# Second MLP product of a hybrid block: moving operand and PSUM result walked in another order of columns, one of eight orders for each bank

## The chip, the cores and the metric

The kernel runs on one core of one Trainium2 chip. The metric is the time of one execution on the device in microseconds (us); smaller is better. The time of the kernel before is the median of three runs.

## The reference, cut to what matters

One layer with parallel heads (an mLSTM group and a differential-attention group) is followed by an MLP. The change touches the last line of the reference only, the product with `w_ff2`:

```python
x = x + (mixed @ w_out[l]).astype(dt)
u = rms(x, norm2_g[l]).astype(dt) @ w_ff1[l]      # 1024 x 4096
u = jnp.square(jax.nn.relu(u))
x = x + (u @ w_ff2[l]).astype(dt)                 # 1024 x 1024
```

Here x is 1024 rows (sequence) by 1024 columns (model width), and `w_ff2` is 4096 by 1024. All is float32.

## The kernel before, in words

The stages follow each other on TensorE: projections, mLSTM, attention, the output projection, the first MLP product (lines 1435 to 1437, program name `m`), and the second MLP product (lines 1764 to 1766, program name `z`). The second MLP product is the last stage.

**How the second product is tiled.** Rows and columns of the result are split into halves, and the four quarter products are formed from seven products of sums and differences, numbered 1 to 7 and worked in the order 1, 6, 2, 5, 7, 3, 4. Each of the seven runs over eight steps j, a step over two blocks b of 128 of the contraction, and a block over four groups n of 128 output rows. So a step has 8 pairs (b, n), and each pair is three matmuls: the weights are cut into a high and a low part (`wh`, `wl`, float32r), the activations too (`gh`, `gl`), and high by high, high by low and low by high are added up. The weights are the stationary operand (128 by 128), the activations are the moving operand (128 partitions by 512 columns), and the result is one PSUM bank, 128 partitions by 512 columns of float32. In all there are 7 x 8 x 2 x 4 x 3 = 1344 matmuls, and each of the three lines issues 448 of them.

**Which bank.** `x = 4 * (i in (6, 5, 3))` chooses the banks: products 1, 2, 7 and 4 add into banks 0 to 3, products 6, 5 and 3 into banks 4 to 7, group n into bank x + n. A bank of 0 to 3 so receives 4 x 8 x 2 x 3 = 192 matmuls and a bank of 4 to 7 receives 3 x 8 x 2 x 3 = 144. Product 2 goes on in the sum of product 1, 3 in that of 5, and 4 in that of 7. A sum in a bank thus runs over 48 or 96 matmuls, and `finish` (lines 1795 and on) then reads the bank with ScalarE or VectorE, column by column, combines it with other sums, and the result goes out.

**The order of the work.** It is written out by hand: `when(t, f, ...)` collects a time in units of the schedule and a function, and the functions are called in order of time, so each engine's queue is in that order. For each step, `fetch` loads the activations from device memory (SyncE's queue), `cut_hi` makes the high part on ScalarE (line 1348) and `cut_lo` the low part on VectorE (line 1351), for the activations (`wb`, `we` in turn) and for the weights (`wa0`, `wa1` in turn); `z_step` issues the 24 matmuls.

## Time and profile before

| what | value |
|---|---|
| median of 3 runs | 1246.6 us |
| lowest and highest of them | 1244.84 and 1247.13 us |
| span of the profiled execution, first to last instruction | 1243.3 us |
| TensorE matmul, busy share of the span | 99% (6437 matmuls) |
| VectorE, ScalarE, GpSimd busy share | 67%, 50%, 19% |
| granted TensorE clock, mean | 1.000 |

For the profiled execution the profile gives the span only; the median of the timed runs lies 3.3 us above that span. In the profile the engines are named PE (TensorE's matmuls), PEld (its weight loads), DVE (VectorE), ACT (ScalarE), POOL (GpSimd) and SP (SyncE). A matmul's own duration is modelled at its end and overlaps the next matmul, so the pace of TensorE is read from the starts of successive matmuls. A row of a group reads: line, engine, operation, result<-operands, shapes, count, then busy time in us and mean ns of one, then the idle time of the engine before them and what ended it.

### The profile page before, as it was taken

The page shows a single profiled execution, that of the slowest core. Times are in us where ns is not written, and L with a number is a line of the kernel's source. Part 1 is how long each engine was busy: PE and PEld are TensorE (multiplying, and loading weights), DVE is VectorE, ACT ScalarE, POOL GpSimd, SP SyncE. Part 2 cuts the span into 40 slices and gives each one's busy share as a digit, 9 for nine tenths or more (in the row PEclk, how much of TensorE's full clock was granted, in tenths as well). Part 3 has the DMA queues.
Part 4 walks back from the last instruction along what each step waited for, and adds up shares of the span by engine and source line. Part 5 has one row for each costly group of instructions (what it writes and reads, how often), then busy time and mean ns, then how long its engine had stood idle before and what let it go on. Part 6 is the DMA issues. An engine that isn't in the chain of part 4 may idle for free. (4 is left out here: it accounts for less than half of the span.)

```text
span 1243.3 us, 17129 instructions
## 1 busy us (share of the span) xinstructions
PE 1235.1 (99%) x6437; PEld 1033.6 (83%) x6437; DVE 827.1 (67%) x1138; ACT 621.4 (50%) x1067; POOL 234.8 (19%) x259
## 2 busy tenths in 40 slices
PE   9999999999999999999999999999999999999998
PEld 8998778888878878888887888888888888888887
DVE  8335658886357786774879886666655874468754
ACT  7223437776455686664455554544534343333332
POOL 0133504564334364322000000000000000004001
PEclk9999999999999999999999999999999999999999
DMA  6404262354275485435544764434359745435632
GB/s 251 153 20 171 52 199 91 111 153 128 93 237 188 150 289 182 160 111 203 173 170 146 257 233 153 162 136 163 144 180 364 260 161 195 139 132 170 221 110 93
DMA packets 101314, 208.31 MB, mean 168 GB/s; under 512 B 8672, under 2 KB 21472, under 8 KB 101232
## 3 DMA queue, kind: packets, MB, share of 16 engines
q1 hardware_dynamic: 77936, 154.11, 37.2%
q10 hardware_dynamic: 15296, 31.89, 6.8%
q0 software_dynamic: 8000, 21.24, 5.2%
q8 instruction: 50, 0.82, 0.3%
q14 instruction: 32, 0.26, 0.1%
HBM read 148.90 MB, written 58.29 MB: 167 GB/s over the span
## 5 line engine op out<-in xcount | busy, mean ns | idle before, releaser
L1809 POOL TENSOR_TENSOR zx<-zx,res 128x512 f32<-128x512 f32 x4 | 8.7, 2179 | 491.0 <-DVE zx L1807 491.0
L1766 PE MATMUL z<-wbh,wa0l 128*128 128x512 f32 x224 | 87.4, 390 | 0.2 <-DVE wa0l L1351 0.2
L1003 DVE CUSTOM_DVE_ANT_0 l<-pl,toe 128x1024 f32<-128x1024 f32 x64 | 76.3, 1221 | 16.6 <-PE pl L998 15.9
L1765 PE MATMUL z<-wbl,wa0h 128*128 128x512 f32 x224 | 87.2, 389 | 0.0
L1765 PE MATMUL z<-wel,wa1h 128*128 128x512 f32 x224 | 87.2, 389 | 0.0
L1764 PE MATMUL z<-weh,wa1h 128*128 128x512 f32 x224 | 87.2, 389 | 0.0
L1764 PE MATMUL z<-wbh,wa0h 128*128 128x512 f32 x224 | 87.1, 389 | 0.0
L1766 PE MATMUL z<-weh,wa1l 128*128 128x512 f32 x224 | 87.1, 389 | 0.0
L1348 ACT ACTIVATE wbh<-g 128x1024 fp32r<-128x1024 f32 x28 | 29.7, 1061 | 90.3 <-PE z L1766 53.0
L1348 ACT ACTIVATE weh<-g 128x1024 fp32r<-128x1024 f32 x28 | 29.7, 1061 | 90.2 <-PE z L1766 53.4
L1009 ACT ACTIVATE l<-l,sm 128x1024 f32<-128x1024 f32 x64 | 73.1, 1148 | 0.5 <-DVE sm L1003 0.5
L1351 DVE TENSOR_TENSOR wel<-g,weh 128x1024 fp32r<-128x1024 f32 x28 | 35.2, 1258 | 56.5 <-ACT weh L1348 56.5
L1484 ACT ACTIVATE sq<-sq 128x512 f32<-128x512 f32 x48 | 30.2, 630 | 82.3 <-DVE sq L1523 65.7
L1351 DVE TENSOR_TENSOR wbl<-g,wbh 128x1024 fp32r<-128x1024 f32 x28 | 35.4, 1265 | 52.4 <-ACT wbh L1348 52.4
L1038 PEld LDWEIGHTS pav<-v,at 128*128 128x128 f32 x512 | 61.5, 191 | 3.4 <-issue 1.1
L1038 PE MATMUL pav<-v,at 128*128 128x128 f32 x512 | 62.7, 275 | 0.0
L998 PE MATMUL pl<-kk,q 64*128 64x512 f32 x384 | 55.3, 410 | 0.9 <-DVE sm L1003 0.9
L136 PE MATMUL pj_c<-hhi,w_c 128*128 128x512 f32 x128 | 53.3, 417 | 0.0
L136 PE MATMUL pw<-mix,hi_wo 128*128 128x512 f32 x128 | 52.0, 406 | 0.0
L138 PE MATMUL pj_c<-hhi,w_c 128*128 128x512 f32 x128 | 50.4, 394 | 0.0
L138 PE MATMUL pw<-mix,lo_wo 128*128 128x512 f32 x128 | 50.1, 391 | 0.0
L137 PE MATMUL pj_c<-hlo,w_c 128*128 128x512 f32 x128 | 50.0, 391 | 0.0
(456 smaller groups left out, 3592.5 us busy)
## 6 DMA issues: line engine op xcount, KB each, us to landing
g<-g_dram SPq DMA_DIRECT2D x56, 512.0 KB, 4.7
g_dram<-gs SPq DMA_DIRECT2D x64, 256.0 KB, 4.3
g_dram<-sq ACTq DMA_DIRECT2D x42, 256.0 KB, 2.1
kk<-k_dram POOLq DMA_DIRECT2D x16, 512.0 KB, 6.3
raw_wo<-in_w_o_dram SPq DMA_DIRECT2D x16, 512.0 KB, 4.5
re<-in_w_dram SPq DMA_DIRECT2D x16, 512.0 KB, 4.3
ro<-in_w_dram SPq DMA_DIRECT2D x16, 512.0 KB, 3.5
zt<-in_w_dram SPq DMA_DIRECT2D x16, 512.0 KB, 4.0
```

What stands on the lines that cost most here:

```text
L136: nc.tensor.matmul(out, ahi, bhi, start=start, stop=False)
L137: nc.tensor.matmul(out, ahi, blo, start=False, stop=False)
L138: latest[0] = nc.tensor.matmul(out, alo, bhi, start=False, stop=stop).ins
L998: nc.tensor.matmul(it.pl[x][:, sl], hd.q[r, i, qi * P : (qi + 1) * P], hd.kk[r, j, sl], start=n == 0, stop=n == 2)
L1003: nc.vector.tensor_tensor_reduce(lt, it.pl[m], hd.toe[:, off : off + S], 1.0, 3.0e38, ALU.add, ALU.min, it.sm[:, m : m + 1])
L1009: nc.scalar.activation(lt, lt, AF.Exp, bias=sm[:, m : m + 1], scale=-1.0, accum_out=sm[:, 2 + m : 3 + m])
L1038: nc.tensor.matmul(it.pav[:, 0:P], at, it.head.v[:, c], start=c == 0, stop=c == NC - 1)
L1348: nc.scalar.activation(dst[0][idx], src, AF.Copy)
L1351: nc.vector.tensor_tensor(dst[1][idx], src, dst[0][idx].bitcast(F32), op=ALU.subtract)
L1764: nc.tensor.matmul(p, wh, gh, start=go, stop=False, skip_group_check=True)
L1765: nc.tensor.matmul(p, wh, gl, start=False, stop=False, skip_group_check=True)
L1766: nc.tensor.matmul(p, wl, gh, start=False, stop=end, skip_group_check=True)
```

## The change: what it does

A helper `walk` is added, and one line in `z_step` puts it around the result `p` and the moving operands `gh` and `gl` of every matmul. The three get the same walk, so a column of the operand still lands in the same place of the bank; only the order in which the 512 columns are streamed differs. The weights, the number of matmuls, their columns and their order are as before.

```diff
+    def walk(t, n):
+
+        if n == 0:
+            return t
+        if n == 5:
+            return t[:, ::-1]
+        if n == 6:
+            return t.rearrange("p (h c) -> p h c", h=4)[:, ::-1]
+        return t.rearrange("p (h a b) -> p a h b", h=2, b={1: 4, 2: 2, 3: 32, 4: 16, 7: 8}[n])
...
             end = j == NJ - 1 and b == 1
+            p, gh, gl = (walk(t, x + n) for t in (p, gh, gl))
             nc.tensor.matmul(p, wh, gh, start=go, stop=False, skip_group_check=True)
```

What a bank's number gives:

| bank | order of the 512 columns | runs of adjacent columns | matmuls |
|---|---|---|---|
| 0 | ascending, as before | 1 of 512 | 192 |
| 1 | halves in turn | 128 of 4 | 192 |
| 2 | halves in turn | 256 of 2 | 192 |
| 3 | halves in turn | 16 of 32 | 192 |
| 4 | halves in turn | 32 of 16 | 144 |
| 5 | descending | 1 of 512, backwards | 144 |
| 6 | four quarters, the last first | 4 of 128 | 144 |
| 7 | halves in turn | 64 of 8 | 144 |

"Halves in turn" with runs of 2 means columns 0, 1, 256, 257, 2, 3, 258, 259 and so on.

On TensorE, at the start of product 1, these matmuls stand before (`z_n` is the bank's tile, `wbh` the high part of the activations, `wa0h` that of the weights; of the three lines of a group only the first is shown):

```order
L1764 MATMUL z_0_8393<-wbh,wa0h 128x512
...
L1764 MATMUL z_1_8394<-wbh,wa0h 128x512
...
L1764 MATMUL z_2_8395<-wbh,wa0h 128x512
...
L1764 MATMUL z_3_8396<-wbh,wa0h 128x512
...
L1764 MATMUL z_0_8393<-weh,wa1h 128x512
```

The same place on TensorE now, and the start of product 6 behind it (`z_0_8684` to `z_3_8687` are its banks 4 to 7):

```order
L1775 MATMUL z_0_8393<-wbh,wa0h 128x512
...
L1775 MATMUL z_1_8394<-wbh,wa0h 128x64x2x4
...
L1775 MATMUL z_2_8395<-wbh,wa0h 128x128x2x2
...
L1775 MATMUL z_3_8396<-wbh,wa0h 128x8x2x32
...
L1775 MATMUL z_0_8684<-wbh,wa0h 128x16x2x16
...
L1775 MATMUL z_1_8685<-wbh,wa0h 128x512
...
L1775 MATMUL z_2_8686<-wbh,wa0h 128x4x128
...
L1775 MATMUL z_3_8687<-wbh,wa0h 128x32x2x8
```

No matmul has moved: the shapes alone differ, and bank 5 keeps the shape 128x512 since its walk is one run backwards. The rows and the waits of VectorE, ScalarE, GpSimd and SyncE are the same as before.

## The prediction

> **What bounds the kernel now.** I read the page's busy times first, then what TensorE waits for, then the last stage by itself, then its tail. The busy line, and the whole list of TensorE's waits for other engines:

> ```profile
> PE 1235.1 (99%) x6437; PEld 1033.6 (83%) x6437; DVE 827.1 (67%) x1138; ACT 621.4 (50%) x1067; POOL 234.8 (19%) x259
> ```

> ```profile
> PE pv L194 <- POOL ones L74: 1.1, 1, 1.1
> PE pl L998 <- DVE sm L1003: 0.9, 2, 0.7
> PE pva L909 <- POOL w_va L643: 0.8, 1, 0.8
> PE m L1435 <- ACT wbh L1348: 0.6, 1, 0.6
> PE pd L764 <- ACT kt L126: 0.4, 1, 0.4
> PE z L1766 <- DVE wa0l L1351: 0.2, 1, 0.2
> ```

> TensorE is the bound: it waits 4.0 us in the whole program, 0.2 us of it in the stage that is changed. So whatever a matmul of this stage gains or loses is gained or lost at the end, one for one, as long as the other engines keep up. The stage by itself, from its first matmul to its last (busy time and instructions of each engine, then the granted clock):

> ```profile
> core 0: us, PE busy (x) PEld busy (x) DVE busy (x) ACT busy (x) POOL busy (x), PEclk, DMA share, GB/s
> 934.00:1239.00 305.00, 304.85 (x1345) 251.75 (x1344) 191.08 (x171) 114.52 (x117) 23.13 (x12) 1.00 0.53 184
> ```

> PE is busy for 304.85 of 305.00 us, at the full granted clock; DVE has 114 us to spare, ACT 190 us. The pace of one matmul is read from starts, here the first and the last of nine successive ones in the middle of the stage, with a few between:

> ```profile
> 1084.38 0.39 PE L1765 MATMUL z<-wel,wa1h 128*128 128x512 f32 x1
> 1084.61 0.39 PE L1766 MATMUL z<-weh,wa1l 128*128 128x512 f32 x1
> 1084.84 0.39 PE L1764 MATMUL z<-weh,wa1h 128*128 128x512 f32 x1
> 1085.06 0.39 PE L1765 MATMUL z<-wel,wa1h 128*128 128x512 f32 x1
> ...
> 1085.97 0.39 PE L1766 MATMUL z<-weh,wa1l 128*128 128x512 f32 x1
> 1086.19 0.39 PE L1764 MATMUL z<-weh,wa1h 128*128 128x512 f32 x1
> ```

> From 1084.38 to 1086.19 are eight starts: 1.81 / 8 = 0.226 us each. Over the stage 305.0 / 1344 = 0.2269 us; I take 227 ns, or 0.443 ns a column. The 0.39 us in these rows is the modelled end, and the next matmul starts long before it. How even the stage is shows in the durations by line (lowest, median, highest in ns):

> ```profile
> L1764 PE MATMUL z<-wbh,wa0h x224: 387/389/396, 934.1 to 1233.3; 128*128 128x512 f32 x112
> L1766 PE MATMUL z<-wbh,wa0l x224: 389/389/497, 934.9 to 1233.7; 128*128 128x512 f32 x112
> ```

> All banks run alike; only the one matmul that waited shows 497. Last, the tail behind the stage:

> ```profile
> 1239.18 0.39 PE L1766 MATMUL z<-weh,wa1l 128*128 128x512 f32 x1
> 1239.68 0.75 DVE L1785 TENSOR_TENSOR zv<-zv,z 128x256 f32<-128x256 f32 x2 [0.67 <-PE z L1766]
> 1240.49 0.33 SPq L1786 DMA_DIRECT2D out_dram<-zv  x1
> ```

> The profiled execution is thus 934.1 us ahead of the stage, 1344 x 0.2269 = 305 us in it, and about 4.2 us of last subtraction and output, 1243.3 us together. That is its span; the profile gives no other time of it. The median of the timed runs, 1246.6 us, lies 3.3 us higher, and I add my terms to the median.

> **What the change removes and adds.** It removes no instruction and adds none; no wait and no order of a queue changes. Its terms are therefore 1344 times the difference in pace between a matmul whose columns are walked one way and the other, bank by bank. Bank 0 (192 matmuls) is as before: nothing. For the other 1152 matmuls no row of this trace is a direct price, as every matmul here walks its columns upwards in one run. So I go by the nearest rows, which are those of engines that read the same two memories.

> *Descending runs.* ScalarE and VectorE read PSUM backwards in the head turns (`zzTrue<-pzTrue`, `mix<-pt`: four runs of 128, each backwards), and forwards elsewhere, with the same work on each element:

> ```profile
> L126 ACT ACTIVATE zzTrue<-pzTrue,cst 128x512 fp32r<-128x512 f32 x8 | 5.4, 685 | 11.6 <-PE pzTrue L364 7.9 <-DVE zzTrue L372 3.7
> L126 ACT ACTIVATE mf<-po,cst 128x512 f32<-128x512 f32 x8 | 5.5, 685 | 15.6 <-PE po L845 13.5 <-DMA raw_o<-in_w_c_dram 2.1
> L372 DVE SCALAR_TENSOR_TENSOR zzTrue<-pzTrue,cst,zzTrue 128x512 fp32r<-128x512 f32 x8 | 5.9, 749 | 12.8 <-ACT zzTrue L126 12.8
> L1383 DVE SCALAR_TENSOR_TENSOR y<-y,cst,r 128x512 f32<-128x512 f32 x16 | 11.0, 747 | 0.0
> ```

> Backwards 685 ns against 685 ns forwards on ACT, 749 against 747 on DVE: the direction is free there.

> *Jumps between runs.* VectorE multiplies four runs of 128 out of a wider tile (`to`, the next run 258 columns on), and elsewhere one run of 512:

> ```profile
> L825 DVE TENSOR_TENSOR to<-to,nd 128x512 f32<-128x512 f32 x8 | 5.5, 693 | 0.5
> L1571 DVE TENSOR_TENSOR ro<-ro 128x512 f32<-128x512 f32 x16 | 11.1, 692 | 0.6
> ```

> 693 against 692 ns: three jumps cost about 1 ns. By these rows banks 5 and 6 cost nothing. For the finer walks (runs of 32 down to 2) I take nothing as well, but that is an extension of the rows, on engines that need a column only every 0.85 ns or more where TensorE takes one every 0.443 ns. So the upper end must be set apart. ScalarE's pace follows from two copies of different length:

> ```profile
> L1348 ACT ACTIVATE wbh<-g 128x1024 fp32r<-128x1024 f32 x28 | 29.7, 1061 | 90.3 <-PE z L1766 53.0 <-issue 36.8 <-PE m L1436 0.5
> L1348 ACT ACTIVATE wbh<-re 128x512 fp32r<-128x512 f32 x20 | 12.5, 625 | 9.2 <-DVE re L1577 5.1 <-ACT sq L1485 3.6 <-DVE wel L1351 0.5
> ```

> (1061 - 625) / 512 = 0.852 ns a column. My upper end for a matmul with an unfavourable walk is that it falls to this pace, about half its own: 512 x 0.852 = 436 ns, or 436 - 227 = 209 ns more. The lower end is nothing: a matmul has 512 columns in any order, and no row shows the pace of 227 ns to hang on the order, so I exclude a gain but for a small chance, priced below. Between the ends I take nothing, since the backward and jumping rows are the only ones that walk memory differently, and all are equal to their plain partners.

> *Cover.* The terms have none: TensorE is busy throughout, so each ns of a slower walk is on the path, and if it slows, DVE and ACT only wait longer. The readers of the banks (`finish`) read whole banks upwards, as before.

> [...]

> **The sum.** 1344 x 0 = 0: 1246.6 us, no change. A measurement of this kernel tells about 0.2% (2.5 us) from nothing; its three runs lie within 2.3 us.

> **The rivals.**

> *Pairs are too short (slower).* Runs of 2 halve the pace, since each pair comes from another place than the one before, while runs of 4 and more still stream. It decides where memory delivers a new place no faster than ScalarE takes two columns. Only bank 2 pays: 192 x 209 ns = 40.2 us, 1286.8 us. For it: TensorE takes columns twice as fast as any engine whose jumps this trace shows. Against it: those jumps are free to 1 ns. [...] Chance 0.17.

> *Every jump costs a column's time (slower).* The address steps out of a run and one beat of 0.443 ns is lost. Jumps in a matmul: 127, 255 and 15 in banks 1 to 3, 31, 3 and 63 in banks 4, 6 and 7. Sum 192 x 397 + 144 x 97 = 90,192 jumps, 40.0 us, 1286.6 us. Against it: three jumps on DVE cost 1 ns, which is no full beat of 0.85 ns each. Chance 0.07.

> *Backwards is slow on TensorE alone (slower).* Bank 5 pays: 144 x 209 ns = 30.1 us, 1276.7 us. Against it the equal 685 ns rows. Chance 0.06.

> *Every walk that isn't one upward run is slow (slower).* All 1152 matmuls pay up to 209 ns: 241 us, 1487 us. [...] Nothing in the trace stands for it, but nothing shows a matmul that could refute it. Chance 0.10, and 0.02 more for odd small costs of a few ns in some bank (3 to 10 us).

> *Faster.* If the pace came down to the shortest step between the starts above, 0.22 us (1085.97 to 1086.19, as rounded there), it would be 7 ns x 1344 = 9 us, 1237 us. I see no reason for it, as the same number of columns passes: 0.03.

> That the change doesn't do what it says can be left out: the shapes of its matmuls are the walks.

> **How the numbers follow.** No change 0.55, pairs 0.17, jumps 0.07, backwards 0.06, all walks 0.10, small costs 0.02, faster 0.03. The likeliest is no change, 1246.6 us. Without the other cases its own range is 1244 to 1249. That holds only 0.55, so the range reaches up over backwards, jumps and pairs to 1288 and leaves out the 0.10 of all walks and the gain: 0.87 inside. The chances: faster 0.03, same 0.55, slower 0.42.

> **What would show it.** Right: starts of successive matmuls 0.227 us apart in every bank, the stage 305 us long at clock 1.00, the same waits of TensorE. Pairs: steps of about 0.44 us in group 2 of products 1, 2, 7 and 4 alone. Jumps: 0.34, 0.28 and 0.25 us in banks 2, 1 and 7 in proportion to their runs. Backwards: group 1 of products 6, 5 and 3 alone. All walks: every group but 0 of products 1, 2, 7 and 4. Wrong altogether: a granted clock below 1.00, or new waits of TensorE, which none of these gives.

## The result, and the profile after

| | before | after |
|---|---|---|
| median | 1246.84 us (4 runs) | 1279.49 us (4 runs, 1278.96 to 1280.46) |
| ratio after to before | | 1.0267, 95% interval 1.0253 to 1.0282 |
| span of the profiled execution | 1243.3 us | 1278.1 us (its own time 1279.84 us) |

The change costs 32.7 us. Two of the seven products of the stage, each from its first matmul to the first of the next: product 2 (banks 0 to 3) and product 5 (banks 4 to 7). A row gives the window in time, its length, then busy time and instructions of each engine and the granted clock. A product has 192 matmuls.

```profile
1032.00:1082.40 50.40, 50.40 (x194) 36.49 (x193) 21.29 (x20) 16.19 (x16) 0.00 (x0) 1.00 0.50 162
1082.40:1127.90 45.50, 45.50 (x194) 36.31 (x193) 23.56 (x22) 16.07 (x16) 0.00 (x0) 1.00 0.42 138
```

50.40 and 45.50 us, where a product took 305.0 / 7 = 43.6 us before. The clock is full, TensorE is busy without a gap, and of its waits only these are listed, none of them at `z`:

```profile
PE pv L194 <- POOL ones L74: 1.1, 1, 1.1
PE pl L998 <- DVE sm L1003: 0.9, 2, 0.6
PE m L1435 <- ACT wbh L1348: 0.6, 1, 0.6
PE m L1435 <- DVE sq L1523: 0.6, 2, 0.3
PE m L1435 <- DVE w L1518: 0.5, 1, 0.5
PE pd L764 <- ACT kt L126: 0.4, 1, 0.4
PE m L1436 <- DVE x4l L1351: 0.3, 1, 0.3
```

The waits at `m` lie ahead of the stage. Three of them, 1.4 us, are not in the list of before, and the stage of this execution begins at 935.6 us in place of 934.1; in the runs below, with the same code ahead of it, it begins between 933.7 and 936.2 us.

So the matmuls themselves are slower. Where, the starts of successive matmuls show; these are groups 3, 0, 1, 2 and 3 of product 1, three matmuls each:

```profile
938.42 0.41 PE L1775 MATMUL z<-wbh,wa0h 128*128 128x512 f32 x1
938.67 0.40 PE L1776 MATMUL z<-wbl,wa0h 128*128 128x512 f32 x1
938.90 0.40 PE L1777 MATMUL z<-wbh,wa0l 128*128 128x512 f32 x1
939.14 0.39 PE L1775 MATMUL z<-wbh,wa0h 128*128 128x512 f32 x1
939.37 0.39 PE L1776 MATMUL z<-wbl,wa0h 128*128 128x512 f32 x1
939.60 0.40 PE L1777 MATMUL z<-wbh,wa0l 128*128 128x512 f32 x1
939.84 0.41 PE L1775 MATMUL z<-wbh,wa0h 128*128 128x512 f32 x1
940.09 0.42 PE L1776 MATMUL z<-wbl,wa0h 128*128 128x512 f32 x1
940.35 0.42 PE L1777 MATMUL z<-wbh,wa0l 128*128 128x512 f32 x1
940.60 0.49 PE L1775 MATMUL z<-wbh,wa0h 128*128 128x512 f32 x1
940.92 0.50 PE L1776 MATMUL z<-wbl,wa0h 128*128 128x512 f32 x1
941.24 0.50 PE L1777 MATMUL z<-wbh,wa0l 128*128 128x512 f32 x1
941.57 0.41 PE L1775 MATMUL z<-wbh,wa0h 128*128 128x512 f32 x1
```

Group 2 (pairs) takes 941.57 - 940.60 = 0.97 us for three, 0.32 us each; group 1 (runs of 4) 0.76 us, 0.25 us each; groups 3 and 0 0.72 and 0.70 us, where three took 0.68 us before. From the differences of all 1344 starts, added up by bank:

| bank | walk | us before | us after | more | mean ns after |
|---|---|---|---|---|---|
| 0 | upwards | 44.07 | 44.95 | 0.9 | 234 |
| 1 | runs of 4 | 43.58 | 48.59 | 5.0 | 253 |
| 2 | runs of 2 | 43.56 | 62.67 | 19.1 | 326 |
| 3 | runs of 32 | 43.32 | 45.58 | 2.3 | 239 |
| 4 | runs of 16 | 32.64 | 34.63 | 2.0 | 240 |
| 5 | backwards | 32.64 | 33.71 | 1.1 | 234 |
| 6 | four quarters | 32.64 | 33.39 | 0.8 | 232 |
| 7 | runs of 8 | 32.64 | 34.86 | 2.2 | 242 |

From 305.1 to 338.4 us this is 33.3 us more, the whole of the loss (the columns are rounded one by one). With the 1.5 us ahead of the stage it makes up the 34.8 us between the two spans. Bank 0, which is walked as before, has become slower too. What is read at these rates, the moving operand or the bank, this table does not say.

### The profile page after: what moved, and what is told of

Its sections match the earlier page's. It is cut to its first block, busy times and chain, and to the rows that moved or that the text cites. A ratio compares the mean times of both kernels' runs of the same rounds, so it can differ in the third digit from the quotient of the medians.

```text
span 1278.1 us, 17130 instructions
## 1 busy us (share of the span) xinstructions
PE 1269.4 (99%) x6437; PEld 1036.5 (81%) x6437; DVE 824.6 (65%) x1138; ACT 621.6 (49%) x1067; POOL 236.6 (19%) x259
## 4 chain that ended last, share of the span: by engine, by line
PE 89%; DVE 4%; DMA 2%; ACT 2%; issue 2%; POOL 1%; ACTq 0%; SPq 0%; DVEq 0%; POOLq 0%
PE z L1776 9%; PE z L1777 9%; PE z L1775 9%; PE m L1435 6%; PE m L1436 6%; PE m L1437 6%; PE pav L1038 4%; PE pva L909 3%; PE pv L248 3%; PE pl L998 3%; PE pw L136 2%; PE pw L138 2%; PE pw L137 2%; PE pa L1026 2%; PE pj_c L136 2%; PE pj_c L138 2%
## 5 line engine op out<-in xcount | busy, mean ns | idle before, releaser
L1776 PE MATMUL z<-wel,wa1h 128*128 128x512 f32 x224 | 93.3, 417 | 0.0
L1776 PE MATMUL z<-wbl,wa0h 128*128 128x512 f32 x224 | 93.2, 416 | 0.0
L1775 PE MATMUL z<-weh,wa1h 128*128 128x512 f32 x224 | 93.2, 416 | 0.0
L1777 PE MATMUL z<-weh,wa1l 128*128 128x512 f32 x224 | 93.2, 416 | 0.0
L1775 PE MATMUL z<-wbh,wa0h 128*128 128x512 f32 x224 | 93.1, 416 | 0.0
L1003 DVE CUSTOM_DVE_ANT_0 l<-pl,toe 128x1024 f32<-128x1024 f32 x64 | 76.3, 1221 | 16.5 <-PE pl L998 15.8
L1348 ACT ACTIVATE weh<-g 128x1024 fp32r<-128x1024 f32 x28 | 29.9, 1068 | 107.4 <-PE z L1777 61.0
L1348 ACT ACTIVATE wbh<-g 128x1024 fp32r<-128x1024 f32 x28 | 29.9, 1066 | 106.3 <-PE z L1777 60.2
L1351 DVE TENSOR_TENSOR wel<-g,weh 128x1024 fp32r<-128x1024 f32 x28 | 34.4, 1227 | 72.8 <-ACT weh L1348 72.8
L1351 DVE TENSOR_TENSOR wbl<-g,wbh 128x1024 fp32r<-128x1024 f32 x28 | 34.8, 1242 | 69.2 <-ACT wbh L1348 69.2
L998 PE MATMUL pl<-kk,q 64*128 64x512 f32 x384 | 55.4, 410 | 0.9 <-DVE sm L1003 0.9
L1777 PEld LDWEIGHTS z<-wbh,wa0l 128*128 128x128 f32 x224 | 42.5, 190 | 14.2 <-DVE wa0l L1351 0.6
L1776 PEld LDWEIGHTS z<-wel,wa1h 128*128 128x128 f32 x224 | 42.6, 190 | 13.9
L1776 PEld LDWEIGHTS z<-wbl,wa0h 128*128 128x128 f32 x224 | 42.6, 190 | 13.9
L1775 PEld LDWEIGHTS z<-weh,wa1h 128*128 128x128 f32 x224 | 42.4, 189 | 14.0
L1777 PEld LDWEIGHTS z<-weh,wa1l 128*128 128x128 f32 x224 | 42.5, 190 | 13.8 <-issue 0.6
```

The source lines that it names most:

```text
L998: nc.tensor.matmul(it.pl[x][:, sl], hd.q[r, i, qi * P : (qi + 1) * P], hd.kk[r, j, sl], start=n == 0, stop=n == 2)
L1003: nc.vector.tensor_tensor_reduce(lt, it.pl[m], hd.toe[:, off : off + S], 1.0, 3.0e38, ALU.add, ALU.min, it.sm[:, m : m + 1])
L1348: nc.scalar.activation(dst[0][idx], src, AF.Copy)
L1351: nc.vector.tensor_tensor(dst[1][idx], src, dst[0][idx].bitcast(F32), op=ALU.subtract)
L1775: nc.tensor.matmul(p, wh, gh, start=go, stop=False, skip_group_check=True)
L1776: nc.tensor.matmul(p, wh, gl, start=False, stop=False, skip_group_check=True)
```

## The experiments

A walk need not go with a bank: any matmul may have its own, since operand and result are walked alike. Most experiments therefore give one walk to each of the seven products, so that 192 matmuls in a row share it, and the pace is the length of that product's window over 192. The helper `walk` then takes the walk itself in place of the bank's number. In the first four runs that is the length of the runs that two halves give in turn, or a name. After them it is a kind and a length of run: `halves` and `quarters` take a run from each of two or four places in turn, `comb` every other run and then the runs left out, `swap` exchanges neighbouring runs, and `blocks` takes the runs in descending order. The two runs on parts of the change keep the change's own helper. Runs without an interval are single runs beside one or more of the kernel before.

**One walk for each product.** In place of the walk by bank:

```diff
-            p, gh, gl = (walk(t, x + n) for t in (p, gh, gl))
+            w = {1: 2, 6: 4, 2: 8, 5: 16, 7: 32, 3: "back", 4: "quarters"}[i]
+            p, gh, gl = (walk(t, w) for t in (p, gh, gl))
```

> One walk for each of the seven products in place of one for each bank, so that 192 matmuls in a row have the same walk: product 1 runs of 2, 6 runs of 4, 2 runs of 8, 5 runs of 16, 7 runs of 32, 3 backwards, 4 quarters. The result is unchanged. Theory A, a jump costs one beat of TensorE (0.42 ns): about 333, 280, 253, 240, 233, 227 and 228 ns from start to start in the seven products, the whole about 39 us over the kernel before. Theory B, only pairs are too short, and what the other banks lost came from standing next to matmuls with another walk: about 326 ns in product 1 and 227 to 229 ns in the other six, about 20 us over. Theory C, every walk other than one upward run has a price of its own that does not depend on neighbours: the medians of the banks after the change, 326, 253, 242, 240, 238, 234 and 232 ns, about 33 us over.

1278.94 us, 33.2 us over the 1245.72 us of before beside it. The seven products in order:

```profile
934.50:998.70 64.20, 64.20 (x193) 37.34 (x192) 27.26 (x26) 17.71 (x19) 0.00 (x0) 1.00 0.70 245
998.70:1046.70 48.00, 48.00 (x193) 36.29 (x192) 33.05 (x28) 18.81 (x20) 0.00 (x0) 1.00 0.42 136
1046.70:1093.50 46.80, 46.80 (x194) 36.43 (x193) 21.29 (x20) 16.10 (x16) 0.00 (x0) 1.00 0.53 176
1093.50:1139.50 46.00, 46.00 (x193) 36.44 (x192) 23.56 (x22) 16.08 (x16) 0.00 (x0) 1.00 0.42 137
1139.50:1185.00 45.50, 45.50 (x194) 36.34 (x193) 34.32 (x28) 16.18 (x16) 16.67 (x8) 1.00 0.45 144
1185.00:1229.80 44.80, 44.80 (x194) 36.09 (x193) 28.09 (x26) 16.06 (x16) 0.00 (x0) 1.00 0.59 182
1229.80:1273.30 43.50, 43.50 (x193) 35.84 (x191) 22.08 (x21) 14.07 (x14) 5.89 (x4) 1.00 0.31 98
```

Over 192: 334, 250, 244, 240, 237, 233 and 227 ns. Pairs stand at theory A's 333 (their 107 ns over 255 jumps are 0.42 ns each), runs of 4 and 8 well below its 280 and 253, and theory B's 227 to 229 holds for the quarters alone. Theory C comes closest, though a little of what a bank shows is its neighbours' (quarters 232 there, 227 here). With these paces the change adds up to 192 x (107 + 23 + 10) + 144 x (17 + 13 + 7 + 0) ns = 32.2 us; the remaining 1 us is what neighbours do to each other, taken together.

**The moving operand alone, and the result alone.**

```diff
-            p, gh, gl = (walk(t, w) for t in (p, gh, gl))
+            gh, gl = (walk(t, w) for t in (gh, gl))
```

> The walks by product as in the run before it, but on the moving operand alone; PSUM is written upwards, so the columns of the result come out permuted and the sums are not the reference's. If the price lies in reading the moving operand from SBUF: the same seven paces as with both walked (about 326 ns in the product with runs of 2). If it lies in writing PSUM: 227 ns in all seven. If each side has a share: in between, and the shares of this run and of the one with PSUM alone add up.

```diff
-            p, gh, gl = (walk(t, w) for t in (p, gh, gl))
+            p = walk(p, w)
```

> The walks by product on the PSUM result alone; the moving operand is read upwards, so the columns of the result come out permuted and the sums are not the reference's. If the price lies in writing PSUM: about 326 ns in the product with runs of 2, as with both walked. If it lies in reading SBUF: 227 ns in all seven products. If each side has a share: the excesses of the two runs add up to that of both walked.

1278.45 and 1245.52 us, beside 1245.72 of before. Products 1 and 6 of the run with the operand walked alone, pairs and runs of 4:

```profile
934.00:998.20 64.20, 64.20 (x193) 37.35 (x193) 27.27 (x26) 17.84 (x19) 0.00 (x0) 1.00 0.71 250
998.20:1046.20 48.00, 48.00 (x193) 36.30 (x192) 33.06 (x28) 18.81 (x20) 0.00 (x0) 1.00 0.40 138
```

And of the run with the result walked alone:

```profile
934.70:978.60 43.90, 43.76 (x194) 35.90 (x193) 26.56 (x26) 17.67 (x19) 0.00 (x0) 1.00 0.96 347
978.60:1022.10 43.50, 43.50 (x194) 36.02 (x192) 33.63 (x29) 18.02 (x20) 0.00 (x0) 1.00 0.47 161
```

64.20 and 48.00 us are those of both walked, to the last digit; 43.90 and 43.50 are those of before within 0.1 us (43.99 and 43.52 by its starts). The whole price lies in reading the moving operand from SBUF (1278.45 us with it walked alone, 1278.94 with both), and the PSUM result took all seven orders at the pace of before (1245.52 us against 1245.72). All of them keep pairs of columns together.

**Neighbours.**

```diff
+            w = (n % 2) * {1: 32, 6: 16, 2: 8, 5: 4, 7: 2, 3: 0, 4: 0}[i]
+            p, gh, gl = (walk(t, w) for t in (p, gh, gl))
```

> Groups 0 and 2 of every product upwards, groups 1 and 3 with runs of 32 in product 1, 16 in 6, 8 in 2, 4 in 5 and 2 in 7; products 3 and 4 upwards throughout. The result is unchanged. If the change of walk between neighbours costs (theory B): the upward groups 0 and 2 stand at 230 to 236 ns in products 1, 6, 2, 5 and 7, and products 3 and 4 at 227 ns. If a price belongs to the walk alone (theories A and C): the upward groups stand at 227 ns everywhere, and the walked groups at the paces of the run with one walk for each product.

1266.27 us beside 1245.72. By the starts, the upward groups stand at 228 to 243 ns (medians by place; one place at 224) wherever groups 1 and 3 are walked, and at 227 ns in products 3 and 4. So an upward matmul behind a walked one loses some ns: here the expectation of theory B holds. That the walked groups keep a price of their own (327 to 340 ns for pairs, 251 to 260 for runs of 4) was theory A's and C's.

**What makes a pair dear: the jump, the distance, or the stretch?** Three theories stood against each other, with walks of the same run length that differ in where the next run lies:

```diff
+            w = {1: ("swap", 2), 6: ("comb", 2), 2: ("swap", 4), 5: ("comb", 4), 7: ("blocks", 4), 3: ("quarters", 2), 4: ("quarters", 4)}[i]
+            p, gh, gl = (walk(t, w) for t in (p, gh, gl))
```

> One walk for each product, moving operand and result both, result unchanged. Product 1: neighbouring pairs swapped (2 3 0 1 6 7 4 5). Product 6: first every other pair upwards, then the pairs left out. Product 2: neighbouring runs of 4 swapped. Product 5: every other run of 4, then the rest. Product 7: runs of 4 in descending order. Product 3: runs of 2 from four quarters in turn. Product 4: runs of 4 from four quarters in turn. So far runs of 2 from two halves cost 333 ns against 227, runs of 4 250. Theory L, what counts is how many pairs are taken from one 16-byte stretch of four columns before it is left: product 1 stays at 227 to 233 ns, products 6 and 3 stand at 333, products 2, 5, 7 and 4 at 227 to 250. Theory J, any jump after a pair costs a beat: products 1, 6 and 3 all at 333 ns, products 2, 5, 7 and 4 at 250. Theory R, what costs is going to and fro between places 1 KB apart: products 1, 6, 2, 5 and 7 at 227 to 235 ns, products 3 and 4 at 333 and 250.

1342.68 us. The seven products:

```profile
935.10:979.10 44.00, 43.85 (x194) 35.99 (x193) 26.66 (x26) 17.73 (x19) 0.00 (x0) 1.00 0.98 352
979.10:1066.10 87.00, 87.00 (x194) 39.78 (x193) 33.63 (x29) 17.99 (x20) 0.00 (x0) 1.00 0.27 94
1066.10:1110.90 44.80, 44.80 (x194) 35.92 (x193) 21.29 (x20) 16.07 (x16) 0.00 (x0) 1.00 0.46 158
1110.90:1155.70 44.80, 44.80 (x194) 36.10 (x193) 23.56 (x22) 16.06 (x16) 0.00 (x0) 1.00 0.44 141
1155.70:1200.50 44.80, 44.80 (x194) 36.10 (x193) 34.35 (x28) 16.23 (x16) 16.56 (x8) 1.00 0.47 144
1200.50:1285.60 85.10, 85.10 (x194) 39.69 (x192) 28.09 (x26) 16.09 (x16) 0.00 (x0) 1.00 0.31 98
1285.60:1337.00 51.40, 51.40 (x193) 37.27 (x191) 23.15 (x21) 14.36 (x14) 7.07 (x4) 1.00 0.25 82
```

Neighbouring pairs swapped: 44.00 us, 227 ns at the median, with a jump after every pair. Every other pair, always upwards and only four columns on: 87.00 us, 453 ns, twice the time of before and dearer than the pairs of the change. So theory J falls by the first row, and theory R by the second. Theory L, the 16-byte stretch of four columns, orders them rightly, but 333 was too little for the second and the sixth row (453 and 443 ns), and too little for the last (268 ns against at most 250).

**Longer runs and descending pairs.**

```diff
+            w = {1: ("comb", 32), 6: ("comb", 16), 2: ("quarters", 8), 5: ("blocks", 2), 7: ("halves", 64), 3: ("halves", 128), 4: ("comb", 8)}[i]
+            p, gh, gl = (walk(t, w) for t in (p, gh, gl))
```

> One walk for each product as before, result unchanged. Product 1: every other run of 32 columns, then the rest; product 6: the same with runs of 16; product 4: with runs of 8; product 2: runs of 8 from four quarters in turn; product 5: pairs in descending order; products 7 and 3: runs of 64 and 128 from two halves in turn. Two halves in turn cost 243, 240 and 237 ns with runs of 8, 16 and 32, and four descending quarters 227. Theory L (columns taken from one 16-byte stretch): product 5 takes two pairs from each stretch and stays near 233 ns, and all others stand below 235 ns. Theory J (each jump costs): product 5 stands at 333 ns, products 4 and 2 at 243, 6 at 240, 1 at 237, 7 and 3 between 227 and 235. Theory R (to and fro between far places): products 1, 6 and 4 near 227 ns, product 2 at 243, products 7 and 3 at 227 to 235; product 5 near 227.

1254.86 us, 9.2 us over the 1245.69 us of before (median of 7). By the starts 237, 236, 231, 233, 227, 227 and 233 ns (medians, in the order of the products; in product 6 236 and 244 by turns, 240 on average). Pairs in descending order, two from each stretch, cost 7 ns: L again and not J. L had products 1 and 6 below 235, though, which J put rightly at 237 and 240. Quarters with runs of 8 are cheaper (231) than halves with runs of 8 (244), and none of the theories has a reason for that.

**Does it matter where a run starts?** The moving operand is shifted by two columns, so that a run of four lies over two stretches:

```diff
+            w, o = {1: (("halves", 4), 0), 6: (("halves", 4), 2), 2: (("comb", 4), 2), 5: (("up", 0), 2), 7: (("comb", 8), 2), 3: (("swap", 2), 2), 4: (("halves", 2), 2)}[i]
+            first = b * (HB - 2 * o) + o
+            gh, gl = (t.rearrange("p b c -> p (b c)")[:, first : first + HB] for t in g_part(s)[0])
+            p, gh, gl = (walk(t, w) for t in (p, gh, gl))
```

> The moving operand starts two columns later in block 0 and two earlier in block 1 (but for product 1), so that a run of 4 no longer is one 16-byte stretch but lies over two; the columns so meet the wrong block of weights and the result is not the reference's. Walks by product: 1 runs of 4 from two halves in turn, not shifted; 6 the same shifted by 2; 2 every other run of 4, shifted; 5 upwards, shifted; 7 every other run of 8, shifted; 3 neighbouring pairs swapped, shifted; 4 runs of 2 from two halves in turn, shifted. Theory L (a visit to a 16-byte stretch takes the time of four columns, unless it is one of the last two stretches read): 250, about 443, about 450, 227, about 333, about 443 and 333 ns in the order of this list. Rival, only the length of a run and the jump behind it count, not where it starts: 250, 250, 233, 227, 233, 227 and 333 ns.

1375.26 us. Products 1, 6, 2 and 3:

```profile
933.90:982.30 48.40, 48.31 (x193) 36.21 (x192) 27.25 (x26) 18.54 (x19) 0.00 (x0) 1.00 0.91 322
982.30:1046.00 63.70, 63.70 (x194) 38.09 (x192) 33.13 (x29) 17.97 (x20) 0.00 (x0) 1.00 0.35 120
1046.00:1133.00 87.00, 87.00 (x193) 39.95 (x192) 21.29 (x20) 16.05 (x16) 0.00 (x0) 1.00 0.25 86
...
1240.90:1306.40 65.50, 65.50 (x193) 37.90 (x192) 28.09 (x26) 16.04 (x16) 0.00 (x0) 1.00 0.36 114
```

The same runs of 4 from two halves go from 252 ns to 332 ns by a shift of two columns, every other run of 4 from 233 to 453, and swapped pairs from 227 to 341. The rival (only run length and jump count) falls. Theory L is right on where a run starts and missed one detail: for products 6 and 3 it had 443 ns, with the last two stretches kept at hand. With the last three kept, both come to 333; four cannot be, since pairs from four quarters in turn (443 ns) find nothing kept. Upwards and shifted, product 5 took 232 ns where both theories had 227.

| walk | beats over 512 | by the rule, ns | measured, ns |
|---|---|---|---|
| neighbouring pairs swapped | 0 | 227 | 227 |
| pairs, two halves in turn | 256 | (sets the beat) | 334 |
| the same, shifted by 2 | 256 | 334 | 329 |
| runs of 4, two halves, shifted by 2 | 256 | 334 | 332 |
| every other run of 8, shifted by 2 | 256 | 334 | 330 |
| swapped pairs, shifted by 2 | 256 | 334 | 341 |
| pairs, four quarters in turn | 512 | 441 | 443 |
| every other pair | 512 | 441 | 453 |
| every other run of 4, shifted by 2 | 512 | 441 | 453 |

The rule stays within 12 ns of these rows. The number three was fitted to two of them and was not tried on a new walk. For every walk that takes whole stretches the rule gives 227 ns, and those took 227 to 268: a second price, which the rule does not have. Two columns taken from each stretch are dear in this matmul of 4-byte columns (every other pair, 453 ns), and with four most of the price is gone (every other run of 4, 233 ns).

**The weights.** A matmul of 512 columns takes 227 ns, which is 13 ns over 512 beats of 0.42 ns, the estimate above. A theory was that the weights' 32 stretches take beats from the moving operand. The weights are read with a step:

```diff
+            step = {1: 4, 6: 2, 2: 1, 5: 4, 7: 4, 3: 1, 4: 1}[i]
+            first = n // step * step * P + n % step
+            nn = slice(first, first + step * (P - 1) + 1, step)
+            wh, wl = (t[:, b, nn] for t in z_part(s)[0])
+            w = {5: ("halves", 4), 7: ("comb", 4)}.get(i, ("up", 0))
+            p, gh, gl = (walk(t, w) for t in (p, gh, gl))
```

> The stationary operand is taken with a step: group n takes every 4th (step 4) or every 2nd (step 2) column of the weights, so that the rows of the result come out in another order and it is not the reference's. Product 1 step 4, product 6 step 2, product 5 step 4 with the moving operand and result in runs of 4 from two halves in turn (250 ns by itself), product 7 step 4 with every other run of 4 (233 ns by itself), products 2, 3 and 4 as before. If the weight load reads SBUF at the moving operand's cost (the 13 ns that a matmul of 512 columns takes over 512 beats being its 32 stretches of 16 bytes): 267 ns in product 1, 240 in 6, 290 in 5, 273 in 7. If it reads on its own and stays hidden: 227, 227, 250 and 233 ns.

1255.38 us. Products 1 and 6 (step 4 and step 2):

```profile
934.40:980.00 45.60, 45.47 (x193) 45.16 (x193) 26.78 (x26) 17.76 (x19) 0.00 (x0) 1.00 0.94 338
980.00:1024.90 44.90, 44.90 (x194) 37.12 (x194) 33.53 (x29) 18.01 (x20) 0.00 (x0) 1.00 0.48 156
```

238 and 234 ns, not 267 and 240; products 5 and 7 253 and 238, not 290 and 273. The load of the weights itself grows longer, as its rows over the whole stage show (lowest, median and highest ns, then the first and last start):

```profile
L1786 PEld LDWEIGHTS z<-wbh,wa0h x224: 187/193/330, 934.2 to 1243.4; 128*128 128x128 f32 x112
```

A load takes 188 ns in products 2, 3 and 4, 193 ns with step 2 and 310 ns with step 4, yet only 3 to 11 ns of that show in the pace. The theory falls, and the load is not wholly hidden either; what the 13 ns are stays open.

**What is left for whole stretches.** Many walks that fill their stretches still cost 4 to 41 ns: in the change the runs of 4, 8, 16 and 32. The second place was moved away by other distances:

```diff
+            hop = {1: 256, 6: 260, 2: 264, 5: 272, 7: 288, 3: 320, 4: 384}[i]
+            first = b * (2 * HB - hop - 256)
+            gh, gl = (
+                bass.AP(tensor=t.tensor, offset=t.offset + first, ap=[t.ap[0], [4, 64], [hop, 2], [1, 4]])
+                for t in (x[:, 0] for x in g_part(s)[0])
+            )
+            p = walk(p, ("halves", 4))
```

> What is left of the price of walks that take whole 16-byte stretches. All seven products read runs of 4 from two places in turn, but the second place lies a hop further on: 256 columns (64 stretches) in product 1, 260 (65) in 6, 264 (66) in 2, 272 (68) in 5, 288 (72) in 7, 320 (80) in 3 and 384 (96) in 4. Columns of the other block of weights are read for that, so the result is not the reference's. Theory B, two stretches a whole power of two apart stand in each other's way in SBUF: 250 ns at a hop of 64 stretches, and 227 to 233 ns at 65 or 66, with the price coming back as the hop nears a large power of two (80 and 96 close to 250). Rival, the price belongs to each jump, wherever it goes: 250 ns in all seven.

1273.33 us; means of 252, 252, 243, 241, 242, 250 and 250 ns. The price depends on the distance, so the rival falls; 65 stretches cost as much as 64, so theory B falls as well, though 64, 80 and 96 are the dear ones beside it. What this second price comes from stays open.

**Parts of the change.** Bank 2 upwards again, and bank 2 alone in pairs:

```diff
-            p, gh, gl = (walk(t, x + n) for t in (p, gh, gl))
+            p, gh, gl = (walk(t, 0 if x + n == 2 else x + n) for t in (p, gh, gl))
```

> The change with one part undone: bank 2 is walked upwards again, the other seven keep their walks. If the pairs carry most of the loss, by their steady pace: 192 x 106.7 ns = 20.5 us of about 33 go, and the kernel stands about 12.5 us (1.0%) above the one before. If the pairs are the only cause (pairs rival): no difference from before. If every walk has the same share: 29 of 33 us stay.

```diff
-            p, gh, gl = (walk(t, x + n) for t in (p, gh, gl))
+            p, gh, gl = (walk(t, 2 if x + n == 2 else 0) for t in (p, gh, gl))
```

> One part of the change alone: bank 2 in pairs, the other seven upwards. If the prices of the walks add up: 20.5 us (1.6%) above the kernel before, and a little more, up to 2 us, for the upward neighbours of the pairs. If the pairs are the only cause of the loss: about 33 us above.

Without the pairs 1260.45 us, ratio 1.012 (1.0105 to 1.0135), 14.8 us over the 1245.69 of before, where 12.5 was expected. The pairs alone 1268.03 us, ratio 1.0179 (1.0162 to 1.0196), 22.3 us, where 20.5 to 22.5 was. The pairs are the largest part but not the only one. The two sum to 37.1 us, 4.4 more than the change, since neighbours set each other's pace. In the first run bank 2 stands at 235 ns though upward; in the second its pairs stand at 334 ns between upward neighbours, in the change at 326. These are 1.5 us each.

**Another eight orders.** To see whether eight orders as such cost anything:

```diff
+            w = (("up", 0), ("swap", 2), ("halves", 64), ("halves", 128), ("blocks", 128), ("swap", 128), ("blocks", 64), ("quarters", 64))[x + n]
+            p, gh, gl = (walk(t, w) for t in (p, gh, gl))
```

> Another eight orders, one for each bank, that take whole 16-byte stretches and jump seldom or near: bank 0 upwards, 1 neighbouring pairs swapped, 2 and 3 runs of 64 and of 128 from two halves in turn, 4 and 6 runs of 128 and of 64 in descending order, 5 neighbouring runs of 128 swapped, 7 runs of 64 from four quarters in turn. The result is unchanged. If what counts is how often a 16-byte stretch is visited: about 227 ns in every bank, the whole within 2.5 us (0.2%) of the kernel before. If any order other than upwards, or the change of order between neighbours, has a price of its own, as the 4 to 9 ns of the upward bank after the change could mean: 4 to 9 ns in each of 1344 matmuls, 5 to 12 us (0.4 to 1.0%) above.

1244.66 us against 1245.23, ratio 0.9998 (0.9989 to 1.0007). Products 6 and 2, over all eight banks:

```profile
977.70:1021.20 43.50, 43.50 (x194) 36.03 (x192) 33.63 (x29) 18.01 (x20) 0.00 (x0) 1.00 0.47 161
1021.20:1064.70 43.50, 43.50 (x193) 36.05 (x192) 21.28 (x20) 16.09 (x16) 0.00 (x0) 1.00 0.55 189
```

43.50 us a product, as before. These eight orders cost nothing, and neither does the change from one to the next, so another order than upwards has no price as such. The upward matmuls of the runs above lose time beside walks that have a price.

## Why the prediction was wrong, point by point

- **TensorE is the bound and nothing covers a slower matmul: right.** The stage grew by 33.3 us by the starts, the time by 32.7 us, with no new wait at `z` and the clock at 1.00.
- **Backwards and quarters cost nothing: right within about 1 us.** In steady state 233 and 227 ns, 144 x 6.6 ns = 1.0 us and none; in the change the two banks lost 1.1 and 0.8 us. So the rival that put 30.1 us on bank 5 fails.
- **"For the finer walks (runs of 32 down to 2) I take nothing as well": the step that failed.** Measured in steady state: pairs 192 x 107 ns = 20.5 us, runs of 4 192 x 23 = 4.4, of 8 144 x 17 = 2.4, of 16 144 x 13 = 1.9, of 32 192 x 10 = 1.9. All of it lies in reading the moving operand. The rows behind the nothing had runs of 128 columns, and those are free for TensorE too (227 ns): they say nothing of shorter runs, on any engine. They were also of ScalarE and VectorE, at a column in 0.85 ns or more. A stretch of four columns needs 4 x 0.42 = 1.7 ns, in which ScalarE, at 0.852 ns each, takes two columns and TensorE four; by this estimate a pair from each stretch would be enough for ScalarE, but no run walks it or VectorE in pairs. By the estimate the stretches account for the pairs; the 10.6 us of the runs of 4 to 32 are measured, and their cause stays open.
- **The pairs rival: right in place, wrong in size and scope.** 209 ns were put on each matmul, ScalarE's pace; the runs showed 107 ns for two halves in turn, where by the reading above half of the pairs come from a stretch still kept, and 216 to 226 ns where none does. It also had runs of 4 and more free and so all the loss in bank 2, which has 19.1 of 33.3 us.
- **The jumps rival: near in numbers, wrong in cause.** It had 0.34, 0.28 and 0.25 us for banks 2, 1 and 7, and the trace after shows 0.33, 0.25 and 0.24. Its whole was 40.0 us against 33.3. By that profile alone it looked nearly right. Swapped pairs, with 255 jumps at 227 ns, refute it.
- **The rival of all walks: wrong in size.** Every walked bank did lose time, but 0.8 to 19.1 us each, and four quarters lose none in steady state. With the result alone walked no walk has a price: 1245.52 us against 1245.72.
- **The range** reached to 1288 us on account of the pairs and the jumps, about 40 us each, and so held 1279.49 us. That is luck: neither cause holds as it was put, and no case had a price for the pairs and smaller ones for the other walks together. The likeliest case was the wrong one, and 0.42 for slower was too little.

## What to carry to other kernels

Before taking a price of nothing from a row, compare what it walked and how fast: a row of long runs on a slow reader (0.852 ns a column) gave no bound for short runs on a reader twice as fast (0.443). When a matmul's columns must come out in another order, walk the PSUM result, which was free in all seven orders tried (1245.52 us against 1245.72), and read the 4-byte moving operand in whole, aligned runs of four columns: these cost at most 41 ns a matmul, where walks that break up the stretches cost 102 to 226, and swapped pairs and the runs of 64 and 128 that were tried cost nothing. And a pattern of prices that fits a theory is worth one experiment that keeps the theory's cause and takes away its rival's: the swapped pairs had every jump and none of the price (227 ns).

## What the runs showed of the hardware that was not expected

- A walk with a price slows the upward matmuls behind it: in the change bank 0 went from 227 ns to 230 to 236 ns, in a pattern that is the same at every repetition. How it is handed on was not found.
- A weight load with step 4 takes 310 ns in place of 188, more than the 238 to 253 ns from one matmul to the next, and still adds only 3 to 11 ns to that pace.
- Runs of 4 from two places cost 23 to 25 ns at a distance of 64, 65, 80 or 96 stretches and 14 to 17 ns at 66, 68 and 72.
